# Time mixing, second part: the small products of a pair's two heads written alternately, chunk by chunk, and tied in pairs

## The chip, the cores and the metric

One core of one Trainium2 chip runs the kernel. The metric is the device time of one execution in microseconds (us), as the median of several executions. TensorE is called PE below, VectorE DVE, ScalarE ACT, GpSimd POOL, SyncE SP.

## What is computed

One layer of a decoder trunk for a prompt of 256 tokens and for 8 samples of 4 tokens, 288 token columns in all, with 2048 features. The change touches one step of it, the time mixing: 16 heads of 64, each with a 64 x 64 state that is carried from token to token.

```python
def wkv7_scan(S0, r, w, k, v, kk, b):
    def step(S, inp):
        r_t, w_t, k_t, v_t, kk_t, b_t = inp
        sa = jnp.einsum('bhij,bhj->bhi', S, -kk_t)
        S = S * w_t[:, :, None, :] + sa[..., None] * b_t[:, :, None, :] + v_t[..., None] * k_t[:, :, None, :]
        y = jnp.einsum('bhij,bhj->bhi', S, r_t)
        return S, y
```

The output y is normalised per head, gets a bonus term and a gate, and goes into the output projection. The final states are outputs too. Everything is in float32.

## The kernel before

The kernel is a sequence of stages over one core: modulation vectors and the input projection, the first part of the time mixing (decays, keys, inverses of small triangular blocks) beside the short convolution, the second part of the time mixing, the output projection, the feed-forward part, and the last norm. The large products are the helper `mm3` (L162 to L165). The change lies in the second part alone, in `second(p, s0r)`, which is called for eight pairs p of heads.

In `second` the recurrence is worked in chunks of 64 tokens: chunks 0 to 3 are the prompt, chunk 4 holds the 32 sample tokens. The two heads of a pair lie on partitions 0 to 63 and 64 to 127 (`half[0]`, `half[1]`, also `LO` and `HI`), so most of the operands of one head cover half of the partitions. The steps, with their lines:

- L811 to L817: five products of keys with reads and removal keys for each head (64 rows, 128 columns), masked by DVE into `AM`.
- L821 to L824 and L829 to L831: five transposes for each head, copied by ACT to `BKt` and `UV`.
- L836 and L849 (32 x 32) complete the inverses `TTbd`; L841 multiplies `AM` with `UV`; L854 turns the removal keys. ACT and DVE copy each result out (L837, L843, L844, L850, L856).
- L860 to L872: the states of the samples are turned (L860), and eight products with 16 columns each (L867) give what they add; four DVE copies put that into `RYs`.
- L875 to L882: the solve with the inverses, into `UV` and `W`.
- L887: what each chunk adds to the state. L895 and L897: a chunk's map from state to state (`MTbd`) and from state to outputs (`RR`).
- L903 to L913: the samples' solve, then the three steps of the state (L912).
- L914 to L923: the reads, into the bank `psY`: for each chunk and head a product with the state (L920), or for chunk 4 with `RYs` (L922), and one with `UV` (L923).
- L926 to L945: the new states. L935 is a product of 512 columns for each head; its operand `UVe` has one buffer.
- From L947 on: group norm, bonus and gate.

In all these steps the loop over the two heads is outside, and the loop over chunks is inside it.

PSUM has eight banks: one for `ada`, three for the tag `acc`, two for `wa` and two for `wb` (`bk(tag)`). Before, each head of a step takes one `acc` bank (two in the first step).

Beside the pairs runs other work: `step(rest)` advances a generator, and each advance loads a piece of 1 MB of modulation weights through SP (one of three `raw` buffers) and multiplies it on PE at L253: four products of 32 columns of weights each, side by side in the columns of the array. Five advances come with each pair, seven with the last one. The states of the next pair (`loads(p + 1)`) are loaded ahead.

No order is written out by hand. A scheduler takes the instructions in the order in which the program issues them, with their data dependences and buffers, and sets a fixed order for each engine when the program is built. Each engine then runs its list in that order and waits on semaphores. `tc.issue_after(x)` says that what follows stands behind x, and `tc.high_priority()` that it is taken first among what is ready.

On PE a float32 product is two passes, each with a weight load (PEld) and a matmul; a transpose is one pass. The trace counts passes, and the order counts products.

Of the kernel before, what the change touches and what calls it, by code (L numbers as in the profile page):

```python
# [1 line left out]

# [13 lines left out]
P = 128  # L16
# [20 lines left out]
# columns of the constant input  # L37
# [10 lines left out]
def shape_constants():  # L48
    """Identity, masks and other tables that the shapes alone determine."""
# [29 lines left out]
def kernel(ctx, tc, i, o):  # L79
# [31 lines left out]
    # sums and deviations within a head: constants that the fast products hold exactly  # L111
# [60 lines left out]
    # activations of the current product, in two parts  # L172
# [20 lines left out]
    if True:  # L193
# [11 lines left out]
        # rows of x, in the place of the products to come  # L205
# [61 lines left out]
    def ada_block(ms, k0, nk):  # L267
        """two modulation vectors at nk feature tiles from k0; four row blocks side by side, then their sum"""
# [25 lines left out]

    def chain(gens):
        for g in gens:
            yield from g
# [16 lines left out]
    def rsqrt_col(q, w, n=1):  # L314
        """last n columns: 1/rms from the first n, sums of squares"""
# [9 lines left out]
    def before(d, a, eng=V):  # L325
        """the row of the token before, less the token's own; the rows before the samples' first lie at the end"""
# [14 lines left out]
    with actx:  # L341
        w_in = i['w_in'][0]

# [81 lines left out]
            # the next blocks' modulation beside the products of each piece  # L425
# [87 lines left out]
        # one room for both parts of the time mixing, so that the second can begin while the first ends  # L513
# [27 lines left out]
        if True:  # L541
# [15 lines left out]
            def lerp(n, p):  # L557
                """between a token's row and the one before, in place"""
# [36 lines left out]
                # decay products within a chunk  # L595
# [17 lines left out]
            def blocks_of(p):  # L613
                """products of removal keys within blocks of 32 (prompt) and of 4 (sample), to one block a partition"""
# [105 lines left out]
        work.close()  # L720
        work = work_pools(0, False)
        with pool("tm2", 2) as wp:
# [3 lines left out]
            # the first pair's first operands lie where tiles above are done with first  # L726
# [9 lines left out]
            RYb = twice([CL, 2, 2, CL], "RYs")  # L736
# [3 lines left out]
            # inverses of the diagonal blocks  # L740
# [4 lines left out]
            def loads(p):  # L745
                """states of the sample"""
# [13 lines left out]
            def second(p, s0r):  # L760
# [9 lines left out]
                # operands side by side  # L770
# [28 lines left out]
                # the places of the operands serve again  # L799
# [18 lines left out]
                for h in range(2):  # L818
                    pt = bk("acc")
                    for c in range(4):  # L820
                        E.transpose(pt[:, c * CL:(c + 1) * CL], BK[half[h], c, h * CL:h * CL + P],  # L821
                                    ident[half[h], half[h]])
                    E.transpose(pt[:, 256:320], BKh[half[h], h * CL:h * CL + P], ident[half[h], half[h]])
                    S.copy(BKt[:, h], v5(pt[:, 0:320]))  # L824
                # values and keys by tokens, inverses of 64 from those of 32
                for h in range(2):
                    pt = bk("acc")
                    for c in range(5):
                        E.transpose(pt[:, c * CL:(c + 1) * CL], vp[half[h], (c + h) * CL:(c + h) * CL + P],  # L829
                                    ident[half[h], half[h]])  # L830
                    S.copy(UV[half[1 - h], h], v5(pt[half[1 - h], 0:320]))  # L831
                for h in range(2):
                    q0, q1 = slice(h * CL, h * CL + 32), slice(h * CL + 32, (h + 1) * CL)
                    ps = bk("acc")
                    for c in range(4):
                        E.matmul(ps[q1, c * 32:(c + 1) * 32], AM[q0, h, c, 32:CL], T1[q0, 4 * p + c], start=True, stop=True)  # L836
                    S.copy(Z[q1], ps[q1, :P].rearrange("p (c t) -> p c t", t=32))  # L837
                for h in range(2):
                    pt = bk("acc")
                    for c in range(5):  # L840
                        E.matmul(pt[half[h], c * CL:(c + 1) * CL], AM[half[1 - h], h, c, 0:CL], UV[half[1 - h], h, c],  # L841
                                 start=True, stop=True)
                    S.copy(AX[half[h], :, 1], v5(pt[half[h], 0:256]))  # L843
                    S.copy(X4[half[h]], pt[half[h], 256:320])  # L844
                for h in range(2):
                    q0, q1 = slice(h * CL, h * CL + 32), slice(h * CL + 32, (h + 1) * CL)
                    ps = bk("acc")
                    for c in range(4):
                        E.matmul(ps[q0, c * 32:(c + 1) * 32], Z[q1, c], TTbd[q1, c, q1], start=True, stop=True)  # L849
                    S.copy(TTbd[q0, 0:4, q1], ps[q0, :P].rearrange("p (c t) -> p c t", t=32))  # L850
                for h in range(2):
                    pt = bk("acc")
                    for c in (1, 2, 3):
                        E.transpose(pt[:, c * CL:(c + 1) * CL], AR[half[h], 0, (c - h) * CL:(c - h) * CL + P],  # L854
                                    ident[half[h], half[h]])
                    V.tensor_copy(AX[half[h], 1:4, 0], v5(pt[half[h], CL:256]))  # L856
                # what the states give the sample
# [8 lines left out]
                for b in range(NB):  # L866
                    E.matmul(ps[LO, b * 16:(b + 1) * 16], S0T[:, b], ARbd[:, b].rearrange("p h y t -> p (h y t)"),  # L867
                             start=True, stop=True)
                for h in range(2):
                    for y in range(2):  # L870
                        V.tensor_copy(s4(RYs[:, h, y, 0:32]),
                                      ps[LO, 0:P].rearrange("p (b z t) -> p z b t", z=4, t=TS)[:, 2 * h + y])  # L872
                # solved for the removal keys and for what the chunk itself gives
# [9 lines left out]
                # a chunk's map from state to state, what it adds, its map from state to outputs  # L883
# [381 lines left out]
```

## Time and profile before

| | us |
|---|---|
| median of three executions (1750.81 to 1753.61) | 1752.29 |
| span of the profiled execution | 1754.8 |
| the stage of the change within it, 483.8 to 757.5 us | 273.7 |
| PE busy over the whole span | 1699.5 (97%) |
| DVE, ACT, POOL busy over the whole span | 1163.6, 713.2, 387.2 |

The profiled execution is one execution, and its span is 2.5 us over the median. PE's busy time counts from the start of a matmul to a modelled end, and matmuls overlap: what a run of matmuls costs is read from its start to the start of the row behind it. The stage begins with the first product of pair 0 and ends where the large products of the output projection begin.

### The profile page before, as it was taken

How to read it: one execution, taken by the hardware profiler on the slowest of the kernel's cores; microseconds unless marked ns; L12 is line 12 of the kernel's file. 1: busy time of each engine (PE TensorE's matmuls, PEld its weight loads, DVE VectorE, ACT ScalarE, POOL GpSimd, SP SyncE). 2: the span in 40 equal slices, each digit the busy share in tenths (PEclk: the TensorE clock that was granted, in tenths of full speed). 3: DMA queues.
4: the chain of work that ended last, by engine and by line, in shares of the span. 5: the costliest groups of instructions: out<-in, count | busy, mean ns of one | idle time of the engine just before them, and what ended most of it. 6: DMA issues, size and time to landing. Idle time of an engine off the chain costs nothing.

```text
span 1754.8 us, 32398 instructions
## 1 busy us (share of the span) xinstructions
PE 1699.5 (97%) x12713; PEld 1507.8 (86%) x12713; DVE 1163.6 (66%) x2480; ACT 713.2 (41%) x1281; POOL 387.2 (22%) x853
## 2 busy tenths in 40 slices
PE   6999999999899999999999999999999999999996
PEld 3778898889866555579899999999999999999996
DVE  3588788976835444445486767576675757667586
ACT  3543355343333232234374443434344343434444
POOL 2121111222623122010033221213122121312212
PEclk9999999999979999999999999999999999999998
DMA  8888855677566465585565554444554455454442
GB/s 264 278 301 278 294 189 189 221 248 235 165 173 207 161 200 178 188 297 168 157 200 168 168 165 159 161 165 150 186 165 159 161 164 169 145 191 159 158 142 73
DMA packets 238304, 333.61 MB, mean 190 GB/s; under 512 B 35697, under 2 KB 180825, under 8 KB 229545
## 3 DMA queue, kind: packets, MB, share of 16 engines
q1 hardware_dynamic: 234937, 324.55, 56.1%
q0 software_dynamic: 2848, 6.20, 1.3%
q8 instruction: 100, 1.64, 0.4%
q10 hardware_dynamic: 368, 0.79, 0.1%
q14 instruction: 51, 0.42, 0.1%
HBM read 321.63 MB, written 9.89 MB: 189 GB/s over the span
## 4 chain that ended last, share of the span: by engine, by line
PE 86%; DVE 8%; ACT 2%; DMA 2%; POOL 1%; issue 1%; SPq 0%; DVEq 0%; ACTq 0%
PE acc L163 21%; PE acc L165 21%; PE acc L164 21%; PE ada L253 5%; DVE wlo L155 2%; PE ada L281 2%; PE acc L814 1%; ACT whi L153 1%; PE wb L935 1%; PE wb L923 1%; DMA A<-in_x_sample_dram 1%; PE acc L841 1%; PE wa L887 1%; PE wa L895 1%; PE wa L912 0%
## 5 line engine op out<-in xcount | busy, mean ns | idle before, releaser
L163 PE MATMUL acc<-actH,whi 128*128 128x288 f32 (+1 forms) x2368 | 706.2, 299 | 7.2 <-DVE ws L689 3.8
L165 PE MATMUL acc<-actH,wlo 128*128 128x288 f32 (+1 forms) x2368 | 700.5, 297 | 3.1 <-DVE wlo L155 3.0
L164 PE MATMUL acc<-actL,whi 128*128 128x288 f32 (+1 forms) x2368 | 703.1, 297 | 0.1
L155 DVE TENSOR_TENSOR wlo<-raw,whi 128x1024 fp32r<-128x1024 f32 (+1 forms) x391 | 480.3, 1230 | 216.2 <-ACT whi L153 205.9
L153 ACT CAST whi<-raw 128x1024 fp32r<-128x1024 f32 x400 | 417.6, 1048 | 479.8 <-PE acc L164 410.8
L163 PEld LDWEIGHTS acc<-actH,whi 128*128 128x128 f32 x2368 | 448.0, 189 | 19.0 <-issue 9.0
L165 PEld LDWEIGHTS acc<-actH,wlo 128*128 128x128 f32 x2368 | 447.4, 189 | 6.1 <-DVE wlo L155 5.2
L164 PEld LDWEIGHTS acc<-actL,whi 128*128 128x128 f32 x2368 | 447.7, 189 | 0.5 <-DVE actL L160 0.3
L163 PE MATMUL acc<-gH,whi 128*128 128x288 f32 x704 | 209.1, 297 | 1.7 <-DVE rd L1036 1.7
L165 PE MATMUL acc<-gH,wlo 128*128 128x288 f32 x704 | 210.4, 299 | 0.0
L164 PE MATMUL acc<-gL,whi 128*128 128x288 f32 x704 | 205.8, 292 | 0.0
L1129 POOL COPY uO<-ub 128x2 f32<-128x2 f32 x88 | 24.7, 280 | 547.4 <-ACT ub L1127 547.4
L163 PEld LDWEIGHTS acc<-gH,whi 128*128 128x128 f32 x704 | 132.3, 188 | 3.7 <-PE acc L165 3.7
L164 PEld LDWEIGHTS acc<-gL,whi 128*128 128x128 f32 x704 | 134.0, 190 | 0.0
L165 PEld LDWEIGHTS acc<-gH,wlo 128*128 128x128 f32 x704 | 132.0, 188 | 0.8
L253 PE MATMUL ada<-raw,cT 128*32 128x512 f32 x512 | 109.9, 610 | 0.6 <-DMA raw<-in_ada_w_dram 0.6
L1034 DVE SCALAR_TENSOR_TENSOR xT<-acc,modT,xT 128x256 f32<-128x256 f32 x192 | 91.7, 477 | 27.5 <-PE acc L165 27.5
L1134 DVE SCALAR_TENSOR_TENSOR uz<-ub,cw,uz 128x304 f32<-128x304 f32 x176 | 96.5, 548 | 4.3
L1126 POOL COPY ub<-sF 128x16 f32<-128x16 f32 x88 | 72.0, 819 | 100.9 <-ACT sF L1030 100.9
L1132 DVE TENSOR_SCALAR uz<-ub,cw 128x304 f32<-128x304 f32 x88 | 33.1, 376 | 49.5 <-ACT ub L1128 49.5
L449 DVE TENSOR_TENSOR A<-acc,A 128x296 f32<-128x296 f32 x96 | 44.3, 463 | 28.9 <-PE acc L165 28.2
L1127 ACT COPY ub<-acc 128x256 f32<-128x256 f32 x84 | 31.8, 378 | 75.8 <-PE acc L165 75.8
(432 smaller groups left out, 1943.1 us busy)
## 6 DMA issues: line engine op xcount, KB each, us to landing
raw<-in_ada_w_dram SPq DMA_DIRECT2D x88, 1024.0 KB, 5.1
raw<-in_ffn_up_dram SPq DMA_DIRECT2D x88, 1024.0 KB, 5.1
raw<-in_w_in_dram SPq DMA_DIRECT2D x48, 1024.0 KB, 6.8
raw<-in_ffn_down_dram SPq DMA_DIRECT2D x44, 1024.0 KB, 5.0
raw<-in_w_out_dram SPq DMA_DIRECT2D x16, 1024.0 KB, 6.7
raw<-in_ada_w_dram SPq DMA_DIRECT2D x16, 512.0 KB, 8.2
dX<-xT SPq DMA_DIRECT2D x1, 2304.0 KB, 15.5
xT<-dX POOLq DMA_DIRECT2D x4, 576.0 KB, 10.1
```

The source lines that it names most:

```text
L153: S.copy(hi, raw)
L155: (GP if cur['share'] and cur['turns'] % cur['share'] == 0 else V).tensor_tensor(lo, raw, hi.bitcast(F32), SUB)
L163: E.matmul(acc, wh, xh, start=start, stop=False)
L164: E.matmul(acc, wh, xl, start=False, stop=False)
L165: E.matmul(acc, wl, xh, start=False, stop=stop)
L253: E.matmul(ps[32 * g:32 * g + 32], cT[:, k, :], raw[:, 512 * g:512 * g + 512], start=(k == 0), stop=(k == KT - 1))
L281: E.matmul(ps[32 * g:32 * g + 32, :n * P], cT[:, k, :], raw[:, :, k % kc], start=(k < 4), stop=(k >= KT - 4))
L449: V.tensor_tensor(A[:, t, 2:LW], acc[:, :NL], A[:, t, 2:LW], ADD)
L1034: V.scalar_tensor_tensor(xT[:, t, :T0], acc[:, :T0], modT[:, m, t, 0:1], xT[:, t, :T0], MUL, ADD)
L1126: GP.tensor_copy(bv[:, :, 0:2], sF[:, :, j].rearrange("p (b t) -> p b t", t=2))
L1132: V.tensor_scalar(z[:, :NC - 2], b[:, 0:NC - 2], cw[:, 0, j:j + 1], None, MUL)
L1134: V.scalar_tensor_tensor(z[:, :NC - 2], b[:, t:NC - 2 + t], cw[:, t, j:j + 1], z[:, :NC - 2], MUL, ADD)
```

## The change

The loop over chunks comes outside and the two heads inside it, in every step of the list above that had the heads outside. Each head has a bank of its own where the two heads lie on different rows of the array (`ps = [bk("acc"), bk("acc")]`). A helper issues the first head's product, and then the second head's with the two calls named above:

```diff
+    def side_by_side(*calls):
+        ins = calls[0]().ins
+        with tc.issue_after(ins), tc.high_priority():
+            for c in calls[1:]:
+                c()
+
+    def mm(*a, start=True, stop=True):
+        return partial(E.matmul, *a, start=start, stop=stop)
```

The first step, as the pattern for the others:

```diff
-                for h in range(2):
-                    H = half[h]
-                    psA, psS = bk("acc"), bk("acc")
-                    for c in range(5):
-                        cc = slice(c * CL, (c + 1) * CL)
-                        E.matmul(psA[:, c * P:(c + 1) * P] if c < 4 else psS[:, 0:P], BK[H, c, h * CL:h * CL + P],
-                                 AR[H, :, cc], start=True, stop=True)
-                    V.tensor_tensor(AM[:, h, 0:4], psA.rearrange("p (c t) -> p c t", t=P), exf(C('map'), 4), MUL)
-                    V.tensor_tensor(AM[:, h, 4], psS[:, 0:P], C('mas'), MUL)
+                ps, px = [bk("acc"), bk("acc")], [bk("acc"), bk("wa")]
+                for c in range(5):
+                    cc = slice(c * CL, (c + 1) * CL)
+                    side_by_side(*[mm(ps[h][:, c * P:(c + 1) * P] if c < 4 else px[h][:, 0:P],
+                                      BK[half[h], c, h * CL:h * CL + P], AR[half[h], :, cc]) for h in range(2)])
+                for h in range(2):
+                    V.tensor_tensor(AM[:, h, 0:4], ps[h].rearrange("p (c t) -> p c t", t=P), exf(C('map'), 4), MUL)
+                    V.tensor_tensor(AM[:, h, 4], px[h][:, 0:P], C('mas'), MUL)
```

The samples' eight products go to the two column halves in turn, and `RYs` covers all 128 partitions (before 64), with two DVE copies for four. The products that read it, L903 and L922, have 128 rows for 64 and the constant `i2` for the identity:

```diff
-                for b in range(NB):
-                    E.matmul(ps[LO, b * 16:(b + 1) * 16], S0T[:, b], ARbd[:, b].rearrange("p h y t -> p (h y t)"),
-                             start=True, stop=True)
+                for b in range(0, NB, 2):
+                    side_by_side(*[mm(ps[half[q], b * 8:b * 8 + 16], S0T[:, b + q],
+                                      ARbd[:, b + q].rearrange("p h y t -> p (h y t)")) for q in range(2)])
```

The reads, and the product of 512 columns:

```diff
-                    for h in range(2):
-                        H = half[h]
-                        if 0 < c < 4:
-                            E.matmul(psY[H, cc], St[c][:, H], RR[:, c - 1], start=True, stop=False)
-                        elif c == 4:
-                            E.matmul(psY[H, cc], ident[LO, LO], RYs[:, h, 1], start=True, stop=False)
-                        E.matmul(psY[H, cc], UV[:, h, c], AM[:, h, c, CL:P], start=c == 0, stop=True)
+                    if 0 < c < 4:
+                        side_by_side(*[mm(psY[H, cc], St[c][:, H], RR[:, c - 1], stop=False) for H in half])
+                    elif c == 4:
+                        side_by_side(*[mm(psY[H, cc], i2, RYs[:, h, 1], stop=False) for h, H in enumerate(half)])
+                    side_by_side(*[mm(psY[H, cc], UV[:, h, c], AM[:, h, c, CL:P], start=c == 0)
+                                   for h, H in enumerate(half)])
...
-                for h in range(2):
-                    UVe = wp.tile([P, NB, CL], F32, tag="UVe", name="UVe", bufs=1)
-                    V.tensor_tensor(UVe, exf(UV[:, h, 4], NB), ex(C('bm'), CL), MUL)
-                    E.matmul(ps[half[h]], BKt[:, h, 4], UVe, start=True, stop=True)
+                UVe = [wp.tile([P, NB, CL], F32, tag="UVe", name="UVe") for _ in range(2)]
+                for h in range(2):
+                    V.tensor_tensor(UVe[h], exf(UV[:, h, 4], NB), ex(C('bm'), CL), MUL)
+                side_by_side(*[mm(ps[half[h]], BKt[:, h, 4], UVe[h]) for h in range(2)])
...
-                so = wp.tile([P, NB // 2, P], F32, tag="so", name="so", bufs=1)
+                so = wp.tile([P, NB // 2, P], F32, tag="UVe", name="so")
```

Outside this stage the order of every engine is the one of before, and SP's is the same throughout. In the stage PE has the same 1300 products and transposes. Lines are moved: in the changed kernel L298 is the first call of a tied pair and L301 the second, and L254 is the L253 of before.

PE at the beginning of the stage, pair 0; `acc<-ws 128x128` is the first step. Before:

```order
L757 MATMUL wb<-actH,conr 128x288
L758 MATMUL wb<-actL,conr 128x288
L814 MATMUL acc<-ws 128x128 x10
L860 MATMUL wa<-con,s0r 128x128
L821 MATMUL acc<-con,ws 128x64 x4
```

After:

```order
L772 MATMUL wb<-actL,conr 128x288
L298 MATMUL acc<-ws 128x128
L301 MATMUL acc<-ws 128x128
L298 MATMUL acc<-ws 128x128
L301 MATMUL acc<-ws 128x128
L298 MATMUL acc<-ws 128x128
L301 MATMUL acc<-ws 128x128
L298 MATMUL acc<-ws 128x128
L301 MATMUL acc<-ws 128x128
L298 MATMUL acc<-ws 128x128
L301 MATMUL wa<-ws 128x128
L876 MATMUL wa<-con,s0r 128x128 x3
```

The ten products of five and five became five tied pairs, and the last of the second head goes to a `wa` bank.

PE in pair 1, from the last of what the chunks add (`wa<-ws 64x64`) over the two maps (`wa<-ws,A`) to the samples' solve (`wa<-con,RYs`). Before:

```order
L887 MATMUL wa<-ws 64x64 x8
L923 MATMUL wb<-ws 64x64
L895 MATMUL wa<-ws,A 64x64 x3
L897 MATMUL wa<-ws,A 64x64 x3
L814 MATMUL acc<-ws 128x128
L253 MATMUL ada<-raw,cT 32x512
L895 MATMUL wa<-ws,A 64x64 x3
L897 MATMUL wa<-ws,A 64x64 x3
L253 MATMUL ada<-raw,cT 32x512 x3
L903 MATMUL wa<-con,RYs_5321 64x64 x2
```

After:

```order
L301 MATMUL wa<-ws 64x64
L298 MATMUL wa<-ws,A 64x64 x6
L298 MATMUL acc<-con,ws 128x64
L254 MATMUL ada<-raw,cT 32x512
L301 MATMUL wa<-ws,A 64x64 x6
L298 MATMUL wa<-con,RYs_5321 64x64
L301 MATMUL wa<-con,RYs_5321 64x64
```

The maps' products still stand as six of one head and six of the other, with other work between.

PE at the end of the last pair: the reads of chunk 4 (`wb<-RYs`, `wb<-ws`), the new state (`wb<-con,A`), and the product of 512 columns (`wb<-UVe,ws`). Before:

```order
L922 MATMUL wb<-RYs_5321,con 64x64
L923 MATMUL wb<-ws 64x64
L922 MATMUL wb<-RYs_5321,con 64x64
L923 MATMUL wb<-ws 64x64
L926 MATMUL wb<-con,A 128x128
L1070 MATMUL wa<-con,shO 128x128
L1070 MATMUL wa<-con,coO 128x128
L935 MATMUL wb<-UVe,ws 64x512
L253 MATMUL ada<-raw,cT 32x512
L935 MATMUL wb<-UVe,ws 64x512
L253 MATMUL ada<-raw,cT 32x512 x3
```

After:

```order
L298 MATMUL wb<-RYs_5321,con 64x64
L301 MATMUL wb<-RYs_5321,con 64x64
L298 MATMUL wb<-ws 64x64
L301 MATMUL wb<-ws 64x64
L941 MATMUL wb<-con,A 128x128
L254 MATMUL ada<-raw,cT 32x512 x3
L1085 MATMUL wa<-con,shO 128x128
L1085 MATMUL wa<-con,coO 128x128
L298 MATMUL wb<-UVe,ws 64x512
L301 MATMUL wb<-UVe,ws 64x512
L254 MATMUL ada<-raw,cT 32x512
```

Both the reads and the wide products stand in pairs, and no piece of `ada` lies between the two wide ones.

## Rows read from the trace of the kernel before

**Rows 1.** The page: busy time, share of the span, instructions.

```profile
PE 1699.5 (97%) x12713; PEld 1507.8 (86%) x12713; DVE 1163.6 (66%) x2480; ACT 713.2 (41%) x1281; POOL 387.2 (22%) x853
```

**Rows 2.** Busy time by stretches: length, five engines, granted clock, DMA share, GB/s.

```profile
490.30:511.00 20.70, 20.07 (x139) 15.44 (x142) 7.25 (x22) 4.03 (x14) 4.34 (x19) 0.51 0.57 178
511.00:599.50 88.50, 88.50 (x757) 51.74 (x752) 43.71 (x131) 29.96 (x91) 22.61 (x54) 1.00 0.60 198
599.50:606.50 7.00, 7.00 (x43) 4.77 (x42) 3.77 (x11) 1.02 (x3) 1.16 (x4) 0.51 0.13 55
...
sum 273.70, PE 271.53 PEld 159.09 DVE 130.14 ACT 79.68 POOL 60.02; mean PE 54.31 PEld 31.82 DVE 26.03 ACT 15.94 POOL 12.00
```

**Rows 3.** PE's longest wait from 480 to 760: total, times, longest us.

```profile
PE acc L836 <- DMA T<-dT: 1.0, 1, 1.0
```

**Rows 4.** PE in order of time, pair 2: start us, us, line, passes.

```profile
564.42 1.16 PE L814 MATMUL acc<-ws 64*128 64x128 f32 x8
565.51 1.10 PE L867 MATMUL wa<-ARbd,S0T 128*64 128x16 f32 x16
566.54 0.43 PE L875 MATMUL wa<-AX,ws 128*128 128x64 f32 x2
...
567.63 0.71 PE L814 MATMUL acc<-ws 64*128 64x128 f32 x6
568.27 0.33 PE L923 MATMUL wb<-ws 128*64 128x64 f32 x2
568.53 0.71 PE L814 MATMUL acc<-ws 64*128 64x128 f32 x4
569.17 0.97 PE L887 MATMUL wa<-ws 128*64 128x64 f32 x16
569.97 0.28 PE L923 MATMUL wb<-ws 128*64 128x64 f32 x2
570.18 0.56 PE L895 MATMUL wa<-ws,A 64*64 64x64 f32 x6
570.58 0.51 PE L897 MATMUL wa<-ws,A 64*64 64x64 f32 x6
571.02 1.04 PE L253 MATMUL ada<-raw,cT 128*32 128x512 f32 x2
572.00 0.56 PE L895 MATMUL wa<-ws,A 64*64 64x64 f32 x6
```

**Rows 5.** The same view, reads and wide products of pair 2.

```profile
577.76 0.34 PE L920 MATMUL wb<-XB,A 128*64 128x64 f32 x4
...
578.15 1.06 PE L253 MATMUL ada<-raw,cT 128*32 128x512 f32 x6
...
580.40 0.32 PE L922 MATMUL wb<-RYs,con 64*64 64x64 f32 x2
...
581.42 0.46 PE L829 MATMUL acc<-con,ws 64*128 64x64 f32 x4
...
583.38 1.07 PE L935 MATMUL wb<-UVe,ws 128*64 128x512 f32 x2
584.38 1.06 PE L253 MATMUL ada<-raw,cT 128*32 128x512 f32 x6
585.37 0.34 PE L829 MATMUL acc<-con,ws 64*128 64x64 f32 x2
```

**Rows 6.** The same view, L841 at half clock (pair 0) and at full (pair 1).

```profile
491.26 2.02 PE L841 MATMUL acc<-ws 64*64 64x64 f32 x20
493.21 0.63 PE L849 MATMUL acc<-ws,A 32*32 32x32 f32 x8
...
556.02 1.20 PE L841 MATMUL acc<-ws 64*64 64x64 f32 x20
557.15 0.24 PE L849 MATMUL acc<-ws,A 32*32 32x32 f32 x2
```

**Rows 7.** Copies out of `acc` from 480 to 790: busy us, mean ns, idle before.

```profile
L824 ACT COPY ws<-acc 128x320 f32<-128x320 f32 x16 | 6.7, 424 | 11.3 <-PE acc L823 10.7 <-PE acc L829 0.5
```

More of the change, by code (lines that the diff above doesn't have):

```diff
@@ L1 @@
 from contextlib import ExitStack
+from functools import partial
 import numpy as np
@@ L735 @@
             ARb = twice([P, NB, 2, 2, TS], "ARbd")
-            RYb = twice([CL, 2, 2, CL], "RYs")
+            RYb = twice([P, 2, 2, CL], "RYs")
             for t in TTb + MTb + Cb + ARb + RYb:
@@ L818, in second @@
-                for h in range(2):
[L819 to L824, printed above, removed]
-                for h in range(2):
[L827 to L831, printed above, removed]
@@ L845, in second @@
-                for h in range(2):
[L846 to L850, printed above, removed]
-                for h in range(2):
[L852 to L856, printed above, removed]
+                ps, px = [bk("acc"), bk("acc")], [bk("acc"), bk("wa")]
@@ new lines, in second @@
+                ps = [bk("acc"), bk("acc")]
+                for c in range(5):
+                    side_by_side(*[turn(ps[h][:, c * CL:(c + 1) * CL],
+                                        BK[half[h], c, h * CL:h * CL + P] if c < 4 else BKh[half[h], h * CL:h * CL + P],
+                                        ident[half[h], half[h]]) for h in range(2)])
+                for h in range(2):
+                    S.copy(BKt[:, h], v5(ps[h][:, 0:320]))
+                ps = [bk("acc"), bk("acc")]
@@ new lines, in second @@
+                for c in range(5):
+                    side_by_side(*[turn(ps[h][:, c * CL:(c + 1) * CL], vp[half[h], (c + h) * CL:(c + h) * CL + P],
+                                        ident[half[h], half[h]]) for h in range(2)])
+                for h in range(2):
+                    S.copy(UV[half[1 - h], h], v5(ps[h][half[1 - h], 0:320]))
+                Q0 = [slice(h * CL, h * CL + 32) for h in range(2)]
+                Q1 = [slice(h * CL + 32, (h + 1) * CL) for h in range(2)]
+                ps = [bk("acc"), bk("acc")]
@@ new lines, in second @@
+                for c in range(4):
+                    side_by_side(*[mm(ps[h][Q1[h], c * 32:(c + 1) * 32], AM[Q0[h], h, c, 32:CL], T1[Q0[h], 4 * p + c])
+                                   for h in range(2)])
+                for h in range(2):
+                    S.copy(Z[Q1[h]], ps[h][Q1[h], :P].rearrange("p (c t) -> p c t", t=32))
+                ps = [bk("acc"), bk("acc")]
+                for c in range(5):
+                    side_by_side(*[mm(ps[h][half[h], c * CL:(c + 1) * CL], AM[half[1 - h], h, c, 0:CL],
+                                      UV[half[1 - h], h, c]) for h in range(2)])
@@ new lines, in second @@
+                for h in range(2):
+                    S.copy(AX[half[h], :, 1], v5(ps[h][half[h], 0:256]))
+                    S.copy(X4[half[h]], ps[h][half[h], 256:320])
+                ps = [bk("acc"), bk("acc")]
+                for c in range(4):
+                    side_by_side(*[mm(ps[h][Q0[h], c * 32:(c + 1) * 32], Z[Q1[h], c], TTbd[Q1[h], c, Q1[h]])
+                                   for h in range(2)])
+                for h in range(2):
+                    S.copy(TTbd[Q0[h], 0:4, Q1[h]], ps[h][Q0[h], :P].rearrange("p (c t) -> p c t", t=32))
@@ L858, in second @@
+                ps = [bk("acc"), bk("acc")]
+                for c in (1, 2, 3):
+                    side_by_side(*[turn(ps[h][:, c * CL:(c + 1) * CL], AR[half[h], 0, (c - h) * CL:(c - h) * CL + P],
+                                        ident[half[h], half[h]]) for h in range(2)])
+                for h in range(2):
+                    V.tensor_copy(AX[half[h], 1:4, 0], v5(ps[h][half[h], CL:256]))
                 ps = bk("wa")
@@ L865, in second @@
                 ps = bk("wa")
-                for b in range(NB):
-                    E.matmul(ps[LO, b * 16:(b + 1) * 16], S0T[:, b], ARbd[:, b].rearrange("p h y t -> p (h y t)"),
-                             start=True, stop=True)
-                for h in range(2):
-                    for y in range(2):
-                        V.tensor_copy(s4(RYs[:, h, y, 0:32]),
-                                      ps[LO, 0:P].rearrange("p (b z t) -> p z b t", z=4, t=TS)[:, 2 * h + y])
+                for b in range(0, NB, 2):
+                    side_by_side(*[mm(ps[half[q], b * 8:b * 8 + 16], S0T[:, b + q],
+                                      ARbd[:, b + q].rearrange("p h y t -> p (h y t)")) for q in range(2)])
+                for q in range(2):
+                    V.tensor_copy(RYs[half[q]].rearrange("p h y t -> p (h y) t")[:, :, 0:32]
+                                  .rearrange("p z (b q t) -> p z q b t", q=2, t=TS)[:, :, q],
+                                  ps[half[q], 0:CL].rearrange("p (b z t) -> p z b t", z=4, t=TS))
                 ps = bk("wa")
@@ L884, in second @@
                 ps = bk("wa")
-                for h in range(2):
-                    for c in range(4):
-                        E.matmul(ps[half[h], c * CL:(c + 1) * CL], BKt[:, h, c], UV[:, h, c], start=True, stop=True)
+                for c in range(4):
+                    side_by_side(*[mm(ps[half[h], c * CL:(c + 1) * CL], BKt[:, h, c], UV[:, h, c]) for h in range(2)])
                 for h in range(2):
```

34 lines of the change are left out of this document (13 added, 21 removed).

## The prediction, as it was put down before the run

> **What bounds the kernel now.** I read the page's busy line first, then the busy time by stretches of the stage that changes, then PE's waits, and last PE's instructions in order of time. PE is busy for 97% of the span [rows 1]. In the stage itself, 273.7 us long, the sum row gives PE 271.53 us, DVE 130.14, ACT 79.68 and POOL 60.02 [rows 2]. PE's waits are almost nothing: the longest is 1.0 us, for the DMA of the inverses into T in pair 0 [rows 3]. So the stage is as long as PE's list takes to go through, and a product that gets cheaper there shortens the kernel, as long as nothing else becomes late.
>
> What a product costs there is seen in the order of time, from the start of a row to the start of the next [rows 4, 5]. Three things are to be seen.
>
> First, a run of passes in one place of the array goes at a fixed pace. L895 and L897, twelve passes in one 64 x 64 tile, take from 570.18 to 571.02, 0.84 us; L895 alone, six, takes 0.40. Twelve passes at 0.058 and 0.14 for the run make 0.84. The 16 passes of L867, all in the lower column half, take 1.03 (0.14 + 16 x 0.058 = 1.07). L814 in one row half takes 1.09 for four products and 0.64 for two, so 0.22 for a product and 0.19 for a run [rows 4].
>
> Second, a change of the kind of tile costs the 0.14 again: the reads of chunk 4 alternate between 64 x 64 (L922) and 128 x 64 (L923), four runs of two passes, from 580.40 to 581.42, 1.02 us, which is 4 x (0.14 + 2 x 0.058) [rows 5].
>
> Third, what lies in another place of the array runs beside. The L814 x6 at 567.63 holds three products, which by the order are one of the first head and two of the second, and it takes 0.64, as the two products of one head at 568.53 do [rows 4]. The L920 and L923 at 577.76 are eight passes, four in each column half, and take 0.39 until 578.15, where eight in one place would take 0.60 [rows 5]. Three products at L253 (x6, 0.99) take what one does (x2, 0.98) [rows 4, 5].
>
> **The change part by part.** I counted the runs in the two orders, with the passes of the busier place in each, and priced them with the numbers above.
>
> Wide products (L935): 16 runs of 1.00 become 8 of two, which by L253's pattern take 1.00 too [rows 5]. Gain 8.0.
>
> Fill (L253): the same 168 products stand in 76 runs for 83, since fewer gaps in the list split a group of four; at 0.98 a run [rows 4], gain 6.9.
>
> First products (L814): 75 products one behind the other become 48, in 29 runs for 31. A part stays single, because the second head's bank or its last product, which goes to `wa`, comes later. 27 x 0.22 + 2 x 0.19 = 6.3.
>
> Reads (L920 to L923): 76 runs become 39, and 210 passes one behind the other 154; chunk 4 now has the same kind of tile as chunk 3 before it. 37 x 0.14 + 56 x 0.058 = 8.4.
>
> Samples (L867): 16 passes in one column half become 8 in each, in each of the eight pairs. 8 x 8 x 0.058 = 3.7.
>
> State additions (L887): 0.80 now [rows 4], which is already less than the 1.07 of 16 passes in a row, so the two heads overlap partly. With 8 passes in each half 0.14 + 0.46 = 0.60; gain 8 x 0.2 = 1.6.
>
> L841: 14 runs become 11 and some 143 passes 102, where a run of twenty (1.13, [rows 6]) counts as 17. 3 x 0.14 + 41 x 0.058 = 2.8.
>
> Transposes: they stand in 50 runs for 43, so 1.0 more, less some passes that now overlap: a loss of 0.7.
>
> The maps (L895, L897) still stand as six and six in the order, so 0. The 32 x 32 products, whose two heads stood side by side or nearly so already, 0. The two DVE copies less in each pair are worth nothing, because DVE is idle for half of the stage [rows 2]; the larger `RYs` only makes L903 and L922 cover 128 rows, and passes cost by columns here. The transposed states `so` now share the ring of `UVe`, so that one masked operand of the next pair waits for this pair's output DMAs. Pairs follow each other in about 34 us (273.7 / 8), and a wait of that length is not in sight; if it came, DVE's list behind it and then L935 would be late.
>
> Sum: 8.0 + 6.9 + 6.3 + 8.4 + 3.7 + 1.6 + 2.8 - 0.7 = 37.0 us of PE's list.
>
> Two things are taken off. In pair 0, PE already waits for T [rows 3]; what it saves before that, five first products (1.1) and half of L867 (0.5), goes into that wait: 1.6. And the tied pair needs two of the three `acc` banks at once, so PE will here and there stand before a copy of 0.42 us [rows 7] that was hidden so far. Below it may cost nothing, as now. Above, at each of the seven steps on `acc` (first products, three transposes, L836, L841, L849) one copy, 7 x 0.42 x 8 = 23.7. I take one copy in each pair of heads, 3.4, nearer to the trace, where every such wait is covered.
>
> Then 37.0 - 1.6 - 3.4 = 32 us. The profiled execution, 1754.8, would become 1722.8. It lies 2.5 over the median of the runs, so for the median I forecast 1752.3 - 32 = **1720 us**.
>
> **A rule against it.** Eight passes in two column halves took 0.39 [rows 5], so weight loads of one half go on while the other half multiplies. The Trainium skill (TensorE: Matmul & The Clock Gate, Part 3: Packing small matmuls) says that a weight load overlaps matmuls in flight only when the row group differs. Column halves share their rows, so by that rule L867, L887 and the passes of the reads would gain nothing. The trace speaks against it; it is the fourth rival.
>
> **The rivals.**
>
> *One, the banks decide.* All seven steps wait for a copy: the 23.7 from above for 3.4. Gain 37.0 - 1.6 - 23.7 = 12, time 1740. For it: three banks, two held at once, and a list made when the products were priced as one behind the other. Against it: the order keeps fill and the other pair's work between most steps, and ACT is idle for 70% of the stage [rows 2].
>
> *Two, the clock: slower than before.* In two stretches of 20.7 and 7.0 us the granted clock is 0.51, half of 2.4 GHz, so 1.2 [rows 2]. There twenty passes of L841 take 1.95 us (491.26 to 493.21) for 1.13 at full clock (556.02 to 557.15) [rows 6]: each us of such work costs 0.73 more. If shorter runs and new waits let the clock fall in each pair of heads, the gain of 32 is gone when 44 us more of the work runs at half clock, 5.5 in each pair. With 8 in each, 64 x 0.73 = 47 us, the time is 1752 - 32 + 47 = 1767. Against it: pairs put more work into the same time, and in the 88.5 us between the two stretches, with the same steps, the clock is 1.00 [rows 2].
>
> *Three, more than forecast.* No new wait, and pair 0's part of the gain falls into half clock, where it is worth 1.7 times as much (2 us more): 1752 - 37 + 1.6 - 2, so 1715; with fewer falls of the clock, 1710.
>
> *Four, column halves do not overlap.* Then L867 (3.7), L887 (1.6) and the passes of the reads (3.2) give nothing: gain 32 - 8.5, time 1729.
>
> *Five, nothing changes.* Rivals one and two together eat the gain: 1750 or so.
>
> **How the numbers follow.** 0.2% of the time, 3.5 us, is about what a measurement of this kernel can tell from no change. The forecast, 1713 to 1728, has 0.56; rival one, up to 1742, 0.18; three, below 1713, 0.09; four 0.07; two 0.05; five 0.05. Faster by over 0.2% is forecast, one, three and four: 0.90. Within 0.2% 0.05, slower 0.05. The range 1711 to 1740 holds the forecast, rival four, most of one and half of three.
>
> **What would show it.** In the changed kernel's trace: two first products in about 0.42 as a run and ten in 1.3, the last stretch of reads (chunks 3 and 4) in about 0.6, the two wide products in 1.0, L867's successor in 0.6, fill in fewer runs. The stage should last some 242 us for 273.7, and the stages outside keep their length. PE's waits in it should total under 6 us. If the stage shrinks less, the list of PE's waits tells rival one (ACT and DVE copies out of `acc`), and the granted clock by stretches tells rival two. The prediction is wrong if pairs stand 0.22 apart instead of beginning together, or if waits on copies exceed 10 us.

## The result and the profile after

The changed kernel takes **1725.7 us** (median of 4, 1725.5 to 1726.2); the kernel before, run beside it, 1753.0 (1750.8 to 1758.3). The ratio is 0.984, with a 95% interval of 0.982 to 0.986, so 25 to 32 us are gained. 1720 was forecast, within 1711 to 1740.

Busy time, share and instructions on the page of the changed kernel, against [rows 1]:

```profile
PE 1657.6 (96%) x12713; PEld 1481.7 (86%) x12713; DVE 1161.9 (67%) x2464; ACT 713.0 (41%) x1281; POOL 385.7 (22%) x853
```

PE has the same 12713 passes and is busy 41.9 us less. The span is 1723.8, 31.0 less than in the profile of before. Busy time by stretches, as in [rows 2] (length, five engines, granted clock, DMA share, GB/s): the stage as the prediction cut it, and then its tail, up to the first large product of the output projection:

```profile
483.80:722.20 238.40, 227.74 (x2201) 132.19 (x2200) 130.37 (x364) 79.61 (x245) 61.47 (x148) 0.97 0.66 207
722.20:731.40 9.20, 3.61 (x28) 0.68 (x27) 4.00 (x10) 2.91 (x9) 3.86 (x9) 0.89 1.01 339
```

The same view of the kernel before, for its tail:

```profile
757.50:762.40 4.90, 2.55 (x20) 0.52 (x18) 3.60 (x9) 2.01 (x4) 0.98 (x2) 1.00 0.98 312
```

So the stage went from 273.7 to 238.4 us, and the tail behind it from 4.9 to 9.2. From here on "the stage" includes the tail: from the first row `wb<-actH,conr` of pair 0 to the first `acc<-actH` of the output projection, 279.0 us before and 248.0 after. The difference is the whole 31.0 us; the rest of the kernel kept its length.

PE's waits in the changed kernel from 480 to 765 (total us, times, longest), where [rows 3] began with 1.0 for T, after the 2.4 for the last pair's norm that lies in the tail:

```profile
PE acc L164 <- ACT whi L154: 3.2, 1, 3.2
PE acc L301 <- DMA T<-dT: 2.4, 1, 2.4
PE wb L1085 <- DVE A L986: 2.3, 1, 2.3
PE acc L301 <- ACT ws L838: 2.2, 6, 0.5
PE wa L301 <- DVE ws L898: 1.2, 3, 0.5
PE wa L298 <- DVE RYs L887: 0.8, 2, 0.4
PE wa L928 <- DVE A L929: 0.8, 1, 0.8
PE wa L298 <- ACT S0T L878: 0.7, 1, 0.7
...
PE acc L298 <- DVE ws L830: 0.4, 1, 0.4
...
PE acc L298 <- DMA T<-dT: 0.2, 1, 0.2
```

What the pairs look like on PE, in order of time (start us, us, line, passes); L298 is the first call of a pair, L301 the second. These rows answer [rows 4, 5]: reads and wide products of pair 2, then samples and first products of pair 3:

```profile
571.12 0.27 PE L298 MATMUL wb<-XB,A 128*64 128x64 f32 x1
571.13 0.27 PE L301 MATMUL wb<-XB,A 128*64 128x64 f32 x1
...
571.74 0.33 PE L941 MATMUL wb<-con,A 128*128 128x128 f32 x1
...
573.84 0.64 PE L298 MATMUL wb<-UVe,ws 128*64 128x512 f32 x1
573.84 0.64 PE L301 MATMUL wb<-UVe,ws 128*64 128x512 f32 x1
...
574.85 1.06 PE L254 MATMUL ada<-raw,cT 128*32 128x512 f32 x6
...
585.08 0.23 PE L298 MATMUL wa<-ARbd,S0T 128*64 128x16 f32 x1
585.09 0.23 PE L301 MATMUL wa<-ARbd,S0T 128*64 128x16 f32 x1
...
585.66 0.43 PE L892 MATMUL wa<-AX,ws 128*128 128x64 f32 x2
...
586.75 0.37 PE L298 MATMUL acc<-ws 64*128 64x128 f32 x1
586.75 0.37 PE L301 MATMUL acc<-ws 64*128 64x128 f32 x1
...
587.39 0.33 PE L298 MATMUL wa<-ws 128*64 128x64 f32 x2
```

Both calls start within 0.01 us. The reads of chunks 3 and 4 take 0.62 (571.12 to 571.74), the two wide products 1.01, the samples' 16 passes 0.58, and four first products 0.64 (586.75 to 587.39).

### The profile page after: what moved, and what is told of

It is laid out like the page before. It is cut to its first block, busy times and chain, and to the rows that moved or that the text cites. A ratio compares the mean times of both kernels' runs of the same rounds, so it can differ in the third digit from the quotient of the medians.

```text
span 1723.8 us, 32394 instructions
## 1 busy us (share of the span) xinstructions
PE 1657.6 (96%) x12713; PEld 1481.7 (86%) x12713; DVE 1161.9 (67%) x2464; ACT 713.0 (41%) x1281; POOL 385.7 (22%) x853
## 4 chain that ended last, share of the span: by engine, by line
PE 82%; DVE 9%; DMA 3%; ACT 3%; issue 1%; POOL 1%; SPq 0%; DVEq 0%; ACTq 0%
PE acc L164 21%; PE acc L166 21%; PE acc L165 21%; PE ada L254 5%; DVE wlo L156 2%; PE ada L282 2%; PE acc L298 1%; ACT whi L154 1%; PE wb L298 1%; PE wa L301 1%; DMA raw<-in_w_in_dram 1%; PE wa L298 1%; PE acc L301 1%; DMA A<-in_x_sample_dram 1%; PE wa L928 1%
## 5 line engine op out<-in xcount | busy, mean ns | idle before, releaser
L164 PEld LDWEIGHTS acc<-actH,whi 128*128 128x128 f32 x2368 | 448.3, 189 | 23.2 <-ACT whi L154 11.1
L1144 POOL COPY uO<-ub 128x2 f32<-128x2 f32 x88 | 24.5, 279 | 548.6 <-ACT ub L1142 548.6
L254 PE MATMUL ada<-raw,cT 128*32 128x512 f32 x512 | 100.0, 604 | 0.7 <-DMA raw<-in_ada_w_dram 0.7
L463 DVE TENSOR_TENSOR A<-acc,A 128x296 f32<-128x296 f32 x96 | 44.2, 463 | 30.7 <-PE acc L166 30.1
```

Source lines behind the costliest of these rows:

```text
L164: E.matmul(acc, wh, xh, start=start, stop=False)
L254: E.matmul(ps[32 * g:32 * g + 32], cT[:, k, :], raw[:, 512 * g:512 * g + 512], start=(k == 0), stop=(k == KT - 1))
L463: V.tensor_tensor(A[:, t, 2:LW], acc[:, :NL], A[:, t, 2:LW], ADD)
```

## The experiments

For every run below the stage was cut in the same way. "Half clock" is the part of it with a granted clock of 0.50 or 0.51 (1.2 GHz); "waits" is the time in which PE had ended one instruction and not begun the next. All are of the one profiled execution; the time is the median of several, and the ratio stands against the kernel before in the same sitting.

| kernel | time | ratio, 95% interval | stage | half clock | waits |
|---|---|---|---|---|---|
| before, first profile | 1752.3 | | 279.0 | 34.1 | 4.5 |
| c0: before again | 1754.1 | 0.999, 0.996 to 1.002 | 273.4 | 20.5 | 5.1 |
| changed | 1725.7 | 0.984, 0.982 to 0.986 | 248.0 | 15.6 | 16.3 |
| e1: wide pair alone | 1739.3 | 0.992, 0.989 to 0.994 | 259.3 | 20.5 | 6.7 |
| e5: wide pair undone | 1735.7 | 0.990, 0.988 to 0.992 | 257.4 | 24.2 | 7.5 |
| e2: untied | 1725.1 | 0.984, 0.982 to 0.987 | 245.0 | 22.8 | 11.5 |
| e3: reads undone | 1728.3 | 0.986, 0.984 to 0.988 | 246.8 | 16.1 | 14.0 |
| e6: samples undone | 1730.6 | 0.987, 0.986 to 0.988 | 252.4 | 23.9 | 9.2 |
| e4: maps in `acc` | 1712.7 | 0.977, 0.976 to 0.979 | 232.9 | 13.7 | 10.3 |
| e7: e4, fill moved | 1717.1 | 0.979, 0.977 to 0.981 | 242.5 | 30.7 | 14.8 |
| e10: changed again | 1726.5 | 0.985, 0.982 to 0.989 | 248.9 | 19.9 | 15.2 |
| e8: e4 again | 1718.4 | 0.981, 0.978 to 0.984 | 238.5 | 27.3 | 10.1 |
| e9: e4, untied | 1722.2 | 0.982, 0.978 to 0.986 | 243.7 | 41.0 | 9.5 |

**c0, the kernel before once more**, unaltered.

> The kernel before, unchanged, for a second profile. Theory 'list' (the stage is as long as PE's list): stage 483 to 762 us, 279 us, as in the first profile; the profile of before showed the clock at half for 34 us of the stage, 20.5 of them in pair 0. If that is usual the span is 1754.8 again. Rival 'clock': the first profile was a dear one, and another shows about 10 us less at half clock and a span near 1750; then some 4 of the 31 us between the two profiles are the clock's and not the change's.

The rival came true for the stage: it was 5.6 us shorter than in the first profile. Its windows (c0) and those of the first profile (the second fence) tell why:

```profile
486.30:506.80 20.50, 19.77 (x131) 14.74 (x133) 7.10 (x21) 4.00 (x14) 3.43 (x15) 0.50 0.56 173
506.80:751.80 245.00, 241.75 (x2021) 136.42 (x2015) 120.62 (x348) 73.33 (x220) 52.67 (x121) 1.00 0.61 194
```

```profile
511.00:762.40 251.40, 248.13 (x2023) 139.23 (x2017) 121.22 (x349) 73.39 (x220) 52.55 (x121) 0.97 0.57 189
```

With the same order of instructions the clock fell in pair 0 alone here, and three times more in the first profile, 13.6 us more at half clock for 5.6 us of time. e4 and e8, one kernel in two executions, differ by the same amounts (13.6 and 5.6, with equal waits), so a us at half clock costs 0.41 here. What makes the clock fall in one execution and not in the other stays open. For the terms of the stage below, c0 is the better baseline, since its 20.5 us at half clock lie nearer to the 15.6 of the changed kernel. Its whole span is no typical one: the profiled execution was the fastest of seven (1745.5, median 1754.1), and another 5.6 us of its span were gained outside the stage, nearly all ahead of it.

**e1, the wide pair alone**, and **e5, all but the wide pair**. e1 is the kernel before with this edit, and e5 the changed kernel with it undone:

```diff
+                UVe = [wp.tile([P, NB, CL], F32, tag="UVe", name="UVe") for _ in range(2)]
                 for h in range(2):
-                    UVe = wp.tile([P, NB, CL], F32, tag="UVe", name="UVe", bufs=1)
-                    V.tensor_tensor(UVe, exf(UV[:, h, 4], NB), ex(C('bm'), CL), MUL)
-                    E.matmul(ps[half[h]], BKt[:, h, 4], UVe, start=True, stop=True)
+                    V.tensor_tensor(UVe[h], exf(UV[:, h, 4], NB), ex(C('bm'), CL), MUL)
+                ins = E.matmul(ps[half[0]], BKt[:, 0, 4], UVe[0], start=True, stop=True).ins
+                with tc.issue_after(ins), tc.high_priority():
+                    E.matmul(ps[half[1]], BKt[:, 1, 4], UVe[1], start=True, stop=True)
```

> Before, with only the product of 512 columns of the two heads as a tied pair (two UVe buffers, so in their ring). Theory 'list': 8 us for the eight runs that are gone, and more, since before a piece of fill stood between the two heads' products (its runs fall from 80 to 71 in the order, 0.98 us each): 8 + 8 = 16 us, so 1736 to 1738. Rival 'the prediction's terms': the 6.9 us of fill belong to all pairs together; then 8 to 10 us, 1743 to 1745. Rival 'masks': the second mask on DVE is late and gives half of it back, 1748.

> The changed kernel with only the product of 512 columns in its old form. Theory 'list': slower than the changed kernel by 8 us for the product and 6 to 8 for the fill that stands between the heads again: 1740 to 1742. Rival 'the prediction's terms': 8 us, 1734.

On PE in order of time, e1 and then e5:

```profile
572.13 0.64 PE L935 MATMUL wb<-UVe,ws 128*64 128x512 f32 x1
572.14 0.64 PE L937 MATMUL wb<-UVe,ws 128*64 128x512 f32 x1
...
573.14 0.46 PE L829 MATMUL acc<-con,ws 64*128 64x64 f32 x4
```

```profile
578.65 1.05 PE L254 MATMUL ada<-raw,cT 128*32 128x512 f32 x2
579.63 1.07 PE L950 MATMUL wb<-UVe,ws 128*64 128x512 f32 x2
580.63 1.06 PE L254 MATMUL ada<-raw,cT 128*32 128x512 f32 x6
...
582.84 1.07 PE L950 MATMUL wb<-UVe,ws 128*64 128x512 f32 x2
```

In e1 the wide products' time goes from 16.0 to 8.1 us against c0, and the fill's from 80.8 to 72.7: 16.0 together, for 1.6 more of waits. e5 gives both back (8.0 each). With one `UVe` buffer the second wide product waits for DVE, and a single product of fill stands ahead of the first one and cuts a group of four (x2, then x6). So the fill's gain belongs to the wide pair and not to the other pairs. The tie is not needed for it: e2 below, untied, has 8.1 and 72.7 as well. The second buffer and the neighbouring products were not tried apart. Against the median of the kernel before in the same sitting (1752.2) e1 gains 13 us and e5 keeps 16, so about half of the change's gain comes with this one product. Both times lie between the ranges of theory and rival.

**e2, no tie.** `side_by_side` issues its calls one after the other, nothing more:

```diff
-        ins = calls[0]().ins
-        with tc.issue_after(ins), tc.high_priority():
-            for c in calls[1:]:
-                c()
+        for c in calls:
+            c()
```

> The changed kernel with the products of the two heads written alternately but without the tie (no issue_after, no high priority). Theory 'list': what counts is that the two heads stand near each other; in the order some runs are longer and fewer, others are broken (first products 32 for 29, reads 46 for 39, transposes 37 for 50), which prices within 2 us of the changed kernel: 1725 to 1728. Rival 'the tie': without it the pairs fall apart and the gain of the reads and the first products (14 us) goes: 1738 or more.

1725.1 for 1725.7: the tie is worth nothing that can be measured. The samples' passes, untied (the trace joins rows of one line):

```profile
556.52 0.65 PE L299 MATMUL wa<-ARbd,S0T 128*64 128x16 f32 x16
557.10 0.43 PE L890 MATMUL wa<-AX,ws 128*128 128x64 f32 x2
```

They take 0.58, as when tied. Other pairs fall apart in part: reads (with L903) and first products take 18.9 and 20.2 us of the stage for 16.0 and 17.8, so 5 of the 14 that the rival named are lost. Transposes (15.0 for 17.7), fill and fewer waits (11.5 for 16.3) make up for it. For the time, writing the heads alternately is enough.

**e3, the reads written by heads again**, with `RYs` left on 128 rows:

```diff
-                    if 0 < c < 4:
-                        side_by_side(*[mm(psY[H, cc], St[c][:, H], RR[:, c - 1], stop=False) for H in half])
...
+                    for h, H in enumerate(half):
+                        if 0 < c < 4:
+                            mm(psY[H, cc], St[c][:, H], RR[:, c - 1], stop=False)()
...
```

> The changed kernel with only the reads written as before (for each chunk: state product and value product of one head, then of the other, no tie); the samples' products and RYs stay as changed, so chunk 4 keeps the same kind of tile as chunk 3. The prediction priced the reads at 8.4 us. Theory 'list': most of that came from RYs on 128 rows and from fewer pieces, not from the alternation, since PE let the two column halves overlap in the old order already; the order has 43 runs of reads for 39 and 71 of fill for 73, together 1 us: 1725 to 1728. Rival 'the alternation of the reads': 1732 to 1734.

1728.3, at the upper end of the range for 'list' and 2.6 over the changed kernel, with intervals that overlap. Chunks 3 and 4 in e3:

```profile
571.47 0.34 PE L935 MATMUL wb<-XB,A 128*64 128x64 f32 x4
...
571.76 0.33 PE L937 MATMUL wb<-RYs,con 128*64 128x64 f32 x4
...
572.14 0.33 PE L941 MATMUL wb<-con,A 128*128 128x128 f32 x1
```

0.67 us for 0.62: here the scheduler put four passes of a kind next to four of the other by itself, and the heads overlap. Over the stage L920 to L923, with L903, take 19.1 us in e3, 16.0 in the changed kernel and 25.3 in c0: of the 9.3 gained, 3.1 hang on the alternate writing of the reads.

**e6, the samples as before** (16 passes into one half, `RYs` on 64 rows, four DVE copies):

```diff
-                for b in range(0, NB, 2):
-                    side_by_side(*[mm(ps[half[q], b * 8:b * 8 + 16], S0T[:, b + q],
-                                      ARbd[:, b + q].rearrange("p h y t -> p (h y t)")) for q in range(2)])
+                for b in range(NB):
+                    E.matmul(ps[LO, b * 16:(b + 1) * 16], S0T[:, b], ARbd[:, b].rearrange("p h y t -> p (h y t)"),
+                             start=True, stop=True)
```

> The changed kernel with only the samples' products in their old form (all in the lower column half, RYs on 64 partitions, 64 rows in the products that read it); reads and all other pairs as changed. Theory 'list': 16 passes in a row for 8 (3.8 us), the reads of chunk 4 fall out of the run of chunk 3 and the samples' solve changes the kind of tile (2 to 3 us), three runs of fill more (3 us), less some transposes: 7 to 8 us of list, time 1731 to 1734. Rival 'only the weight loads': 3.7 us, 1729.

```profile
557.57 1.10 PE L883 MATMUL wa<-ARbd,S0T 128*64 128x16 f32 x16
558.61 0.43 PE L890 MATMUL wa<-AX,ws 128*128 128x64 f32 x2
```

1.04 us (557.57 to 558.61) for 0.58, in eight pairs 8.7 for 4.7. The reads, with L903, take 18.2 for 16.0, so 2.2 of their 9.3 hang on the shape of `RYs`. Column halves do overlap, and the fourth rival is out; so is the rule of the Trainium skill that stood behind it (TensorE: Matmul & The Clock Gate, Part 3: Packing small matmuls), for both halves share their rows. In the changed kernel's trace a weight load of one half begins at 585.14, while a matmul of the other half runs from 585.09 to a modelled end at 585.32. The median rose by 4.9 us only, to just under the range expected: the list grew by 11.5 (of which some 3.4 are 8.3 us more at half clock, at 0.41 each), but PE's waits fell by 7.1. What is saved on PE's list comes back in part as waits here; in e4, next, it does not.

**e4, the maps too.** In the changed kernel the two heads' maps share the tag `wa`, which has two banks. PE in order of time, changed kernel:

```profile
559.68 0.91 PE L298 MATMUL wa<-ws,A 64*64 64x64 f32 x12
...
561.98 0.91 PE L301 MATMUL wa<-ws,A 64*64 64x64 f32 x12
562.82 0.34 PE L298 MATMUL acc<-con,ws 64*128 64x64 f32 x2
```

Tied in the code, they stand 2.3 us apart in the list. My theory was that the second head's bank of `wa` is not free when the first head begins. e4 gives the second head another bank:

```diff
-                ps = [bk("wa"), bk("wa")]
+                ps = [bk("wa"), bk("acc")]
```

> The changed kernel with the second head's bank of the two maps (old L895, L897) taken from acc and not from wa, so that both heads' banks can be free at once. In the order the twelve products then alternate (8 runs for 16) in all pairs of heads. Theory 'list': 6.7 us less for the maps and 1.6 for the rest of the list, 8.3 us; if waits stay at 16 us: 1717 to 1719. Rival 'banks': with acc taken once more the other steps on acc wait, waits grow by 5 us or more: 1722 or more.

```profile
558.89 0.27 PE L298 MATMUL wa<-ws,A 64*64 64x64 f32 x1
558.90 0.27 PE L301 MATMUL acc<-ws,A 64*64 64x64 f32 x1
...
559.58 0.22 PE L298 MATMUL wa<-ws,A 64*64 64x64 f32 x1
559.59 0.22 PE L301 MATMUL acc<-ws,A 64*64 64x64 f32 x1
```

The maps go from 13.4 to 7.4 us, and, in the new order, first products and transposes from 35.5 to 29.2 together. Waits fall to 10.3, where 16 were expected, and 1712.7 beats both kernels and the range expected (1717 to 1719). Its waits, first rows:

```profile
PE wb L1085 <- DVE A L986: 2.2, 1, 2.2
PE wa L298 <- ACT ws L897: 1.8, 4, 0.5
PE acc L301 <- DMA T<-dT: 1.6, 1, 1.6
```

The wait for the first large weights (3.2) and those for L838 (2.2) are gone, although `acc` now serves one use more.

**e7, e4 with two advances of fill moved from the last pair to the first two**, to end earlier:

```diff
-                for _ in range(5 if p < NP - 1 else 7):
+                for _ in range(6 if p < 2 else 5):
```

> e4_maps_acc with two of the seven pieces of fill of the last pair moved to the first two pairs (six, six, then five each). Theory 'list and waits': waits at the end of the stage (5.6 us in the changed kernel: 2.3 for the last pair's norm before a product in a bank of that pair, 3.2 for the first weights of the output projection, which wait for a buffer of fill) shrink, because the buffers come free earlier and the list has 12 us less than the changed kernel's: 1713 to 1716. Rival 'cover': with less fill at the end the last pair's chain lies open and the waits there grow by what the list saved: 1718 to 1721.

```profile
PE wb L1085 <- DVE A L986: 4.4, 1, 4.4
```

1717.1, in neither range and not faster than e4; the intervals overlap, and the profiled execution had 17.0 us more at half clock. The fill at the end had covered a part of the last pair's norm; without it that wait is 4.4 for 2.2.

**e10, e8, e9: the changed kernel, e4, and e4 untied, on one chip.**

> The changed kernel once more, unaltered, for its scatter and beside the two runs below. If the gain of 27 us over the kernel before is a property of the kernel and not of one chip's sitting, 1723 to 1729. Half clock in the stage was 15.6 us in its first profile and 13.7 to 30.7 in the variants; each us at half clock costs about 0.4, so a second profile can lie 5 us higher without any other difference.

> The changed kernel with the second head's maps in an acc bank, once more. First measured 1712.7. If that was its shorter list (some 8 us) and not one lucky sitting, 1710 to 1718, and its interval does not touch that of the changed kernel beside it, with maps (L909, L913) again near 7.4 us of PE and waits near 10. If the first run was luck, 1718 to 1726.

> The second head's maps in an acc bank, and no tie: the calls of a pair are issued one after the other and the scheduler places them as it will. If alternate writing and separate banks carry the gain, as the untied run before this one indicated (1725.1 for 1725.7), the time is that of the run beside it within 4 us. If the tie matters once the maps alternate too, slower by 5 us or more.

The changed kernel again took 1726.5 (1720.7 to 1728.8), and e4 1718.4 (1716.4 to 1721.5), 8.1 less; one run of each reaches into the other's range, and the intervals overlap. That is 0.4 over the range expected for e4, and the separate intervals did not come; the maps (8.0, with 27.3 us at half clock) and the waits (10.1) are as in its first profile. Over both sittings e4's eight runs lie from 1712.1 to 1721.5 and the changed kernel's from 1720.7 to 1728.8. So e4 is the fastest version here, by some 8 to 13 us. e9 lies 3.8 over e8, with overlapping ranges and 13.7 us more at half clock, so a worth of the tie is not shown there either.

## Why the prediction was right, and where not

**What bounds the stage** was right: a shorter list on PE shortened the kernel by most of it.

**The list** came out nearly as summed, 37.0 forecast and 36.6 measured. Some 2.0 of that are the clock's, since c0 has 4.9 us more at half clock; e10, the changed kernel with 19.9 us at half clock, lies 34.6 below c0. From the start of a row to the start of the next, waits left out, c0 against the changed kernel:

| kind of product | c0 | changed | less | forecast |
|---|---|---|---|---|
| wide (L935) | 16.0 | 8.1 | 7.9 | 8.0 |
| fill (L253) | 80.8 | 73.7 | 7.1 | 6.9 |
| first products (L814) | 24.0 | 17.8 | 6.2 | 6.3 |
| reads (L920 to L923), with L903 | 25.3 | 16.0 | 9.3 | 8.4 |
| samples (L867) | 8.5 | 4.7 | 3.8 | 3.7 |
| state additions (L887) | 7.6 | 6.4 | 1.2 | 1.6 |
| L841 | 11.1 | 8.7 | 2.4 | 2.8 |
| transposes and 32 x 32 | 26.6 | 27.9 | -1.3 | -0.7 |
| maps (L895, L897) | 14.4 | 13.4 | 1.0 | 0 |
| full array | 54.0 | 54.9 | -0.9 | 0 |

So pricing a run by its change of tile and the passes of its busier place held, and so did reading the overlap of column halves from eight passes in 0.39 us [rows 5]. That passes cost by columns holds between 64 and 128 columns (0.058 and 0.11 us a pass), but the 16 columns of L867 cost 0.058 too [rows 4]. The reasons were less right than the sizes: the prediction put the fill's term down to fewer gaps in the list, and e1 shows that it comes with the wide pair and its second `UVe` buffer. The count itself held: the trace has 73 runs of fill for 80, seven fewer as counted. Of the reads' term e3 and e6 place 3.1 and 2.2; the other 4.0 stayed in both and was not taken apart.

**The step that failed is what was taken off**: 1.6 for T and 3.4 for copies, 5.0 in all. Measured, PE's waits grew from 5.1 to 16.3, by 11.2. The term for T was right (1.0 before, 2.4 and 0.2 after, 1.6 more). The waits within the pairs (the rows of the list but T, the first weights and the last norm) went from 1.5 to 7.4, 5.9 more, and another 0.5 lies in gaps too short for the list. Of these 7.4, waits for a bank that a copy had still to empty are 3.4: 2.2 and 0.4 on `acc` (L838, L830), and 0.8 on `wa` (L887, whose copy into `RYs` the waiting product does not read). c0 has 0.8 of this kind, so 2.6 more came where 3.4 was taken for one copy in each pair: that term was nearly right. What failed is that everything else stood at nothing. Operands that are not ready yet cost 2.7 (L898, L929, `S0T`), in c0 none. That the product that makes an operand and the one that reads it stand closer together is shown for L898: from the last product of the solve to the first that reads its result PE has 0.8 to 2.2 us of other work in c0 and 0.6 to 1.1 in the changed kernel. The remaining 1.3 of the 7.4 lie in pair 0 behind POOL and ACT, for 0.7 in c0. The bound of 23.7 was far off on the other side.

The rest, 3.2, lies where no change was forecast: "the stages outside keep their length" failed at the tail. PE in order of time at the end, changed kernel:

```profile
723.44 1.06 PE L254 MATMUL ada<-raw,cT 128*32 128x512 f32 x8
726.85 0.28 PE L1085 MATMUL wb<-con,coO 128*16 128x128 f32 x1 [2.34 <-DVE A L986]
727.05 1.07 PE L254 MATMUL ada<-raw,cT 128*32 128x512 f32 x8
731.37 0.61 PE L164 MATMUL acc<-actH,whi 128*128 128x288 f32 x1 [3.25 <-ACT whi L154]
```

The first load of output weights was issued at 723.4, and its product starts 8.0 us later; before it was 754.5 and 762.4, 7.9. What shrank is the work within those 8 us: 5.5 us of instructions then (754.5 to 760.0, and after that the same 2.3 us for the norm, in which the weights landed), 2.3 us now. The load goes out when a product of fill gives its buffer free, so its time hangs on where that product stands in PE's list. That a shorter stage alone brings it too late is not shown: e4's stage is 15 us shorter still, but there the load is issued 10.2 us ahead of the first product, and no such wait is left. On the changed kernel an earlier load was not tried.

Then 36.6 - 11.2 = 25.4 us, which is c0's stage less the changed kernel's (273.4 - 248.0), for 32 forecast (e10: 34.6 - 10.1 = 24.5); the medians differ by 27.2.

**The baseline** hid this miss. From the profile of before the sum gave a span of 1722.8, and 1723.8 came out; but that execution had 34.1 us at half clock in the stage and the changed one 15.6, which at 0.41 each makes an estimate of 7.6 of those 31.0 us. That the two spans agree is luck. The prediction also set a span beside a median of times. A time is some 1.7 over its span (the changed kernel's profiled run: 1725.54 and 1723.8), so that execution lay about 4 over the median, not 2.5.

**The rivals.** One (the banks) is the direction in which the forecast missed, but the waits on banks come to 3.4, not 23.7, and the others are of a kind that it did not name. Two (the clock) did not come: 15.6 us at half clock, less than before. Three needed no new waits. Four is refuted by e6, five by the time.

**What would show it.** The short signs all came: 0.62 for the reads, 1.01 for the wide pair, 0.58 for the samples, 0.42 for two first products (from 502.13) and 1.32 for ten (from 483.86), and fewer runs of fill. The stage as cut then was 238.4 for "some 242". The waits, 10.7 in that cut, were over the 6 us named, and those on copies under the 10 that would have refuted it.

## What to carry to other kernels

Price a list of small products by runs: one cost for a change of the kind of tile, and one for each pass of the busier place; what is saved is real, but expect a part of it back as waits once products and the copies between them stand closer (11.2 of 36.6 here, but 5.2 of 45.7 in e4, which also had 6.8 us less at half clock than c0; the part depends on the order that comes out). For two heads to run side by side they need to be written near each other and, where each has a bank of its own, both banks free; a tie added nothing to the time, and a tie on banks that are not free (the maps) did nothing until one bank's tag was changed. Look at the end of the stage for what the removed work had hidden, and profile the baseline twice before counting terms of a few us.

## What was not expected of the hardware

A kernel whose order is fixed showed granted clocks that differ from one execution to the next: 20.5 or 34.1 us at 0.5 in the same stage before, 13.7 or 27.3 in e4 and e8, both times 5.6 us of time for 13.6 us at half clock. Products of two heads in the two column halves of the same 128 rows cost as one, down to 16 columns (16 passes in 0.58 us, for 1.04 in one half).
